# A hybrid decoder layer on one core: half-height score products, a predicated copy, half-width value products, and new homes for three buffers

## The chip, the cores and the metric

One of the eight cores of a Trainium2 chip runs the whole layer. The metric is device time in microseconds; lower is better. TensorE multiplies 128-row by 128-column weight tiles with streams of up to 512 columns into PSUM; VectorE, ScalarE and GpSimd work on 128 partitions; SyncE's queue issues most transfers.

## The reference, cut to what matters

The layer has two sub-layers over 1024 positions of width 1024. The first takes one input projection, and gives part of its columns to four mLSTM heads (a convolution of width 4, then chunks of a matrix memory) and part to eight attention heads of 64 dimensions in two key/value groups, with rotary, a window of 128 positions and a learned sink per head. The second is a gated MLP with a convolution of width 3. Both are modulated by six vectors, which are products of a 1024-vector with `w_ada`, 24 MB of weights in 48 chunks of 128 columns. All of it is float32.

```
kband = concatenate([previous key block, key block])      # 256 keys for 128 queries
s = einsum('bnqgrd,bnkgd->bngrqk', qb, kband) / sqrt(64)
s = where((rel >= 0) & (rel < 128), s, -inf)               # rel = query - key position
m = maximum(max(s), sink);  p = exp(s - m)
p = p / (sum(p) + exp(sink - m))
o = einsum('bngrqk,bnkgd->bnqgrd', p, vband)
```

For each query exactly 128 of the 256 keys are valid: key column c of the previous block where c is above the query's row, and of the own block where it is not.

## The kernel before, in words

The program is written in Python over a tile framework. A planner, with a timeline of its own, sets the order of each engine's instructions; buffers are taken from pools, and an instruction waits until the buffer that it writes is free.

The work goes in this order. `h_chunk` computes the modulated input. A first pass over it gives keys and values (`pkv`) and half the mLSTM values. `kv_evac` applies rotary to the keys, transposes them and splits them into a rounded part `khi` and a rest `klo`, so that three float32r products (`mm3`, lines 88 to 90) give a float32-like product. `token_group(4, ...)` gives values and gates. `att_group(6, 0)` and `att_group(8, 1)` each project queries for eight blocks of 128 positions, four heads at a time, and run `att_front` and, two blocks later, `att_back`. Behind them `conv_chunk` projects q and k of each mLSTM head into `ubq` and `ubk` and convolves them on VectorE, and `ml_head` runs the chunks. Then come the gate `o_group`, the output projection and the MLP.

In `att_front` the queries of two heads (one of each key/value group) lie above each other in 128 rows. `khi` and `klo` have two planes, one a group, each with zeros in the other group's 64 rows. One product of 128 rows and 2 x 256 columns therefore gives the scores of both heads against both key blocks. ScalarE copies them to `raw`, GpSimd clears the invalid half of each block (lines 367 and 368), and VectorE adds the two blocks into `sm` (line 369). Maximum, exponential and sum follow.

In `att_back` the probabilities are transposed. One product takes the whole transposed block with the previous block's values, a second one the part that belongs to the own block with the difference of the two blocks' values (`vdf`). Both have the values of both groups, 128 columns, and line 399 picks the group's 64.

Two buffers meet here. `ada_bg` loads a chunk of `w_ada` during the attention into the buffer `ub` of the pool `wp`, one buffer, and multiplies it on VectorE (line 174); the same buffer later holds `ubq`. `ubk` is in the pool `lp`, which takes the memory of the attention's pools after `ap_.release()` and `kp.release()`.

Of the kernel before, what the change touches and what calls it, by code (L numbers as in the profile page):

```python
# [10 lines left out]
F32 = mybir.dt.float32  # L11
F32R = mybir.dt.float32r
# [6 lines left out]
P = 128  # L19
# [38 lines left out]
def layer_kernel(  # L58
# [19 lines left out]
    def f(ap):  # L78
        return ap.bitcast(F32)
# [7 lines left out]
    def mm3(ps, lh, ll, rh, rl, first, last):  # L87
        T.matmul(ps, lh, rh, start=first, stop=False)  # L88
        T.matmul(ps, lh, rl, start=False, stop=False)  # L89
        T.matmul(ps, ll, rh, start=False, stop=last)  # L90
# [57 lines left out]


    cb = adap.tile([P, D], F32, name="cb")  # L150
    kp = tc.alloc_tile_pool(name="keys", bufs=1, side="right")
    khi = kp.tile([P, 2, S], F32R, name="khi")
    klo = kp.tile([P, 2, S], F32R, name="klo")
    G.memset(f(khi), 0.0)
    G.memset(f(klo), 0.0)
    ap0 = tc.alloc_tile_pool(name="start", bufs=1, side="right")
    xT = ap0.tile([P, KD, S], F32, name="xT")
    crow, cth = (ap0.tile([P, D], F32, tag=f"w{i}", name=n)[0:1, :] for i, n in enumerate(("crow", "cth")))
# [13 lines left out]
    def ada_chunk(j, w):  # L172
        nc.sync.dma_start(w, w_ada[j * P : (j + 1) * P, :])
        V.scalar_tensor_tensor(w, w, 1.0, cb, op0=ALU.mult, op1=ALU.mult, accum_out=mod[:, j : j + 1])  # L174
# [75 lines left out]

    ada_left = list(range(16, 48))

    def ada_bg(pool=None):
        j = ada_left.pop(0)
        ada_chunk(j, pool.tile([P, D], F32, tag="w", bufs=2, name=f"ada{j}") if pool else wp.tile([P, 4 + S], F32, tag="ub", name=f"ada{j}")[:, :D])

    def token_group(u, n, evac):
        (h0, l0), (h1, l1) = units[u], units[u + 1]
# [58 lines left out]
    def kv_evac(b, ps):  # L317
        kr = ap_.tile([P, 256], F32, tag="qr", bufs=2, name=f"kr{b}")
        rope(kr[:, :P].rearrange("p (h t f) -> p h t f", h=2, t=2),
             ps[:, :P].rearrange("p (h t f) -> p h t f", h=2, t=2), b, 2)  # L320
        A.copy(vat[:, b, :], ps[:, P : 2 * P])
        if b:
            V.tensor_tensor(vdf[:, b, :], ps[:, P : 2 * P], vat[:, b - 1, :], op=ALU.subtract)
        pk = pB(f"pk{b}")
        T.transpose(pk[:, :P], kr[:, :P], ident)
        ts = slice(b * P, (b + 1) * P)
        for g in range(2):
            r = slice(64 * g, 64 * g + 64)
            A.copy(khi[r, g, ts], pk[r, :P])
            V.tensor_tensor(klo[r, g, ts], pk[r, :P], f(khi[r, g, ts]), op=ALU.subtract)  # L330

    rsta = cp.tile([P, NB], F32, name="rsta")

    def att_front(gi, b, ps):
        qr = ap_.tile([P, 256], F32, tag="qr", bufs=2, name=f"qr{gi}_{b}")
        rope(qr.rearrange("p (h t f) -> p h t f", h=4, t=2),
             ps[:, :256].rearrange("p (h t f) -> p h t f", h=4, t=2), b, 4)
        pq = pB(f"pq{gi}_{b}")
        for i in range(2):
            T.transpose(pq[:, i * P : (i + 1) * P], qr[:, i * P : (i + 1) * P], ident)  # L340
        qhi = ap_.tile([P, 256], F32R, tag="qhi", bufs=2, name=f"qhi{gi}_{b}")
        qlo = ap_.tile([P, 256], F32R, tag="qlo", bufs=2, name=f"qlo{gi}_{b}")
        A.activation(qhi, pq[:, :256], AF.Copy, scale=0.125)
        V.scalar_tensor_tensor(qlo, pq[:, :256], 0.125, f(qhi), op0=ALU.mult, op1=ALU.subtract)
        den = ap_.tile([P, 4], F32, tag="den", bufs=3, name=f"den{gi}_{b}")
        ngm = ap_.tile([P, 4], F32, tag="ngm", bufs=3, name=f"ngm{gi}_{b}")
        mx = ap_.tile([P, 4], F32, tag="mx", bufs=3, name=f"mx{gi}_{b}")
        es = ap_.tile([P, 4], F32, tag="es", bufs=3, name=f"es{gi}_{b}")

        sinks = rw[:, 8:16].rearrange("p (v j) -> p j v", v=2)[:, 2 * gi : 2 * gi + 2, :]  # L350
        nsk = nsink.rearrange("p (v j) -> p j v", v=2)[:, 2 * gi : 2 * gi + 2, :]

        sm = ap_.tile([P, 4, P], F32, tag="sm", bufs=4, name=f"sm{gi}_{b}")
        kn = P if b == 0 else 2 * P
        ks = slice((b + 1) * P - kn, (b + 1) * P)
        for i in range(2):
            ps_s = pA(f"s{gi}_{b}_{i}")[:, : 2 * kn].rearrange("p (v k) -> p v k", v=2)
            mm3(ps_s, qhi[:, i * P : (i + 1) * P], qlo[:, i * P : (i + 1) * P], khi[:, :, ks], klo[:, :, ks], True, True)
            si = sm[:, 2 * i : 2 * i + 2, :]
            if b == 0:  # L360
                A.copy(si, ps_s)
                G.affine_select(si, si, pattern=[[0, 2], [-1, P]], compare_op=ALU.is_ge, fill=NEG, base=0, channel_multiplier=1)
            else:
                raw = ap_.tile([P, 2, 2 * P], F32, tag="sr", bufs=3, name=f"sr{gi}_{b}_{i}")
                A.copy(raw, ps_s)
                old, new = raw[:, :, :P], raw[:, :, P:]
                G.affine_select(old, old, pattern=[[0, 2], [1, P]], compare_op=ALU.is_ge, fill=0.0, base=-1, channel_multiplier=-1)
                G.affine_select(new, new, pattern=[[0, 2], [-1, P]], compare_op=ALU.is_ge, fill=0.0, base=0, channel_multiplier=1)
                V.tensor_tensor(si, old, new, op=ALU.add)
        V.tensor_reduce(mx, sm, axis=AX.X, op=ALU.max)  # L370
        V.scalar_tensor_tensor(ngm.rearrange("p (j v) -> p j v", v=2), mx.rearrange("p (j v) -> p j v", v=2), -1.0, nsk, op0=ALU.mult, op1=ALU.min)  # L371
        for i in range(4):
            A.activation(sm[:, i, :], sm[:, i, :], AF.Exp, bias=ngm[:, i : i + 1], accum_out=den[:, i : i + 1])  # L373
        V.tensor_tensor(es.rearrange("p (j v) -> p j v", v=2), ngm.rearrange("p (j v) -> p j v", v=2), sinks, op=ALU.add)
        A.activation(es, es, AF.Exp)
        V.tensor_tensor(den, den, es, op=ALU.add)
        V.reciprocal(den, den)
        return sm, den

    def att_back(gi, b, sm, den):  # L380
        pt = pB(f"pt{gi}_{b}").rearrange("p (a b) -> p a b", a=4)
        for i in range(4):
            T.transpose(pt[:, i, :], sm[:, i, :], ident)

        pT = ap_.tile([P, 4, P], F32, tag="pT", bufs=4, name=f"pT{gi}_{b}")
        A.copy(pT, pt)
        pTs = [(pT, vat[:, max(b - 1, 0), :])]
        if b:
            pN = ap_.tile([P, 4, P], F32, tag="pT", bufs=4, name=f"pN{gi}_{b}")
            G.affine_select(pN, pT, pattern=[[0, 4], [1, P]], compare_op=ALU.is_ge, fill=0.0, base=0, channel_multiplier=-1)  # L390
            pTs.append((pN, vdf[:, b, :]))
        po = pC(f"po{gi}_{b}")
        for i in range(4):
            for n, (pT, va) in enumerate(pTs):
                T.matmul(po[:, i * P : (i + 1) * P], pT[:, i, :], va, start=n == 0, stop=n == len(pTs) - 1)

        base = ATT0 + gi * 128
        for v in range(2):
            V.tensor_tensor(
                mix[b][:, base + v * 256 : base + v * 256 + 128].rearrange("p (j d) -> p j d", j=2),  # L400
                po.rearrange("p (j v d) -> p j v d", j=2, v=2)[:, :, v, 64 * v : 64 * v + 64],
                bc(den.rearrange("p (j v) -> p j v", v=2)[:, :, v], 2, [P, 2, 64]),
                op=ALU.mult,
            )
        if gi == 1:
            sq = ap_.tile([P, 4, P], F32, tag="sm", bufs=4, name=f"asq{b}")
            A.activation(sq.rearrange("p a b -> p (a b)"), mix[b][:, ATT0:], AF.Square, accum_out=ssq[:, b : b + 1])
            rstd_of(rsta[:, b : b + 1], ssq[:, b : b + 1], 512)
            G.tensor_scalar(mix[b][:, ATT0:], mix[b][:, ATT0:], rsta[:, b : b + 1], 0.0, op0=ALU.mult, op1=ALU.add)
# [10 lines left out]
    def v_gates(b, ps):  # L420
        v_evac(b, 0, ps[:, :256])
        A.copy(gates.rearrange("p (g b) -> p g b", g=8)[:, :, b], ps[:, 256:264])
        ada_bg()

    for b in range(NB):
        G.memset(mix_v(b)[:, :, HD : HD + 1], vscale)
# [4 lines left out]
    def att_group(u, gi):  # L431
        pending = []

        def ev(b, ps):
            pending.append((gi, b, *att_front(gi, b, ps)))
            ada_bg()
            if len(pending) > 2:
                att_back(*pending.pop(0))

        token_group(u, 256, ev)  # L440
        while pending:
            att_back(*pending.pop(0))
# [84 lines left out]
    def conv_chunk(u, ch, name):  # L527
        hi, lo = units[u]
        hi = hi[:, :1024].rearrange("p (k n) -> p k n", k=8)
        lo = lo[:, :1024].rearrange("p (k n) -> p k n", k=8)  # L530
        ub = (wp if name[0] == "q" else lp).tile([P, 4 + S], F32, tag="ub", bufs=1, name=f"ub{name}")
        V.memset(ub[:, 0:4], 0.0)
        for t in range(2):
            ps = mm(f"cv{name}_{t}")
# [654 lines left out]
```

## Time and profile before

| | |
|---|---|
| median of 3 runs | 1161.43 us (1159.47 to 1161.55) |
| the profiled execution | 1161.49 us, span 1159.1 us |
| TensorE busy | 1114.8 us, 96% |
| VectorE busy | 858.7 us, 74% |
| ScalarE busy | 578.4 us, 50% |
| GpSimd busy | 212.4 us, 18% |
| moved by DMA | 144.72 MB |

The span is the part of an execution that the profiler saw. A row of the timeline says when an instruction started and how long it took; matmuls overlap their neighbours, so their pace is read from one start to the next. PEld is TensorE's weight load. Brackets hold the idle time ahead of an instruction and what ended it.

### The profile page before, as it was taken

Reading aid. Unit: us, or ns where it says so; the run is one execution under the profiler, and the core shown is the slowest. Engines: PE = TensorE matmul, PEld = TensorE weight load, DVE = VectorE, ACT = ScalarE, POOL = GpSimd, SP = SyncE. Lnnn points to the kernel's source line nnn. Section 1 sums busy time; section 2 is a strip of 40 time slices with the busy share of each in tenths; the row PEclk is TensorE's granted clock in tenths of the full one; section 3 lists DMA queues with packets and bytes.
Section 4 is the critical chain, followed back from the end, with each engine's and each line's share of the span. In section 5 each row is a group of like instructions: output and inputs, shape, how many; then the busy total and the mean of one; then the engine's idle time right before and its main releaser. Section 6 shows DMA issues by size and latency. Waiting matters only on the chain.

```text
span 1159.1 us, 16041 instructions
## 1 busy us (share of the span) xinstructions
PE 1114.8 (96%) x5811; PEld 942.3 (81%) x5811; DVE 858.7 (74%) x1529; ACT 578.4 (50%) x1184; POOL 212.4 (18%) x300
## 2 busy tenths in 40 slices
PE   5899989988999999999999999999999999999997
PEld 3898989877899988887788888888888888787885
DVE  6956877459776545789987797878878775787666
ACT  6543456544554535566554454545454555345452
POOL 3011555665577400000000000000000000000021
PEclk9899999999999999999999999999999999999998
DMA  9654330133110512333332333133223358553545
GB/s 345 243 193 157 108 101 2 56 127 109 55 55 1 182 57 89 108 111 105 113 105 77 118 118 107 67 118 118 93 81 109 114 188 287 192 172 119 172 117 200
DMA packets 54161, 144.72 MB, mean 125 GB/s; under 512 B 5265, under 2 KB 5569, under 8 KB 54082
## 3 DMA queue, kind: packets, MB, share of 16 engines
q1 hardware_dynamic: 52208, 138.19, 35.4%
q10 hardware_dynamic: 1874, 5.51, 1.2%
q8 instruction: 45, 0.74, 0.3%
q14 instruction: 34, 0.28, 0.1%
HBM read 115.09 MB, written 28.60 MB: 124 GB/s over the span
## 4 chain that ended last, share of the span: by engine, by line
PE 68%; DVE 6%; DMA 2%; issue 1%; POOL 1%; ACT 1%; SPq 0%; DVEq 0%; POOLq 0%; ACTq 0%
PE X L858 7%; PE X L857 7%; PE X L856 7%; PE Y L858 4%; PE Y L856 4%; PE Y L857 4%; PE y L88 3%; PE y L90 3%; PE y L89 3%; PE Z L858 1%; PE Z L856 1%; PE Z L857 1%; PE dx L1029 1%; PE dx L1028 1%; PE dxu L1030 1%; PE dx L1030 1%
## 5 line engine op out<-in xcount | busy, mean ns | idle before, releaser
L93 POOL TENSOR_SCALAR rsb<-ssb 128x1 f32<-128x1 f32 x4 | 2.3, 584 | 611.0 <-ACT junk L1081 610.8
L174 DVE SCALAR_TENSOR_TENSOR ada<-ada,cb 128x1024 f32<-128x1024 f32 x48 | 65.2, 1365 | 29.0 <-DMA ada<-in_w_ada_dram 29.0
L856 PE MATMUL X<-S,wl 128*128 128x512 f32 x156 | 62.4, 400 | 0.0
L858 PE MATMUL X<-S,wl 128*128 128x512 f32 x156 | 61.9, 396 | 0.0
L857 PE MATMUL X<-S,wl 128*128 128x512 f32 x156 | 61.7, 395 | 0.0
L866 DVE SCALAR_TENSOR_TENSOR yg<-ug,cv,yg 128x1023 f32<-128x1023 f32 (+1 forms) x44 | 56.4, 1281 | 5.7 <-ACT yg L863 5.7
L85 ACT CAST wl<-T 128x512 fp32r<-128x512 f32 x41 | 25.5, 621 | 66.4 <-PE X L857 62.6
L866 DVE SCALAR_TENSOR_TENSOR yv<-uv,cv,yv 128x1023 f32<-128x1023 f32 (+1 forms) x44 | 56.3, 1279 | 1.9 <-ACT yv L863 1.9
L85 ACT CAST w<-T 128x512 fp32r<-128x512 f32 x47 | 29.1, 623 | 40.8 <-PE Z L858 34.7
L85 DVE TENSOR_TENSOR w<-T,w 128x512 fp32r<-128x512 f32 x47 | 32.1, 688 | 16.6 <-ACT w L85 16.6
L85 DVE TENSOR_TENSOR A<-ra,A 128x512 fp32r<-128x512 f32 x46 | 31.6, 687 | 17.0 <-ACT A L85 16.9
L910 DVE TENSOR_TENSOR uv<-q,X 128x512 f32<-128x512 f32 x22 | 15.1, 686 | 38.4 <-PE X L858 38.4
L85 ACT CAST B<-rb 128x512 fp32r<-128x512 f32 x44 | 27.2, 619 | 31.3 <-DMA rb<-in_w_down_dram 13.4
L85 ACT CAST A<-ra 128x512 fp32r<-128x512 f32 x46 | 28.5, 620 | 28.6 <-PE dxu L1030 14.1
L373 ACT ACTIVATE sm<-sm,ngm 128x128 f32<-128x128 f32 x64 | 24.9, 391 | 27.7 <-DVE ngm L371 27.1
L85 DVE TENSOR_TENSOR B<-rb,B 128x512 fp32r<-128x512 f32 x44 | 30.2, 687 | 9.7 <-ACT B L85 9.1
L85 ACT CAST wl<-fu 128x512 fp32r<-128x512 f32 x21 | 13.0, 621 | 47.5 <-PE Y L857 44.5
L858 PE MATMUL Y<-S,wl 128*128 128x512 f32 x92 | 36.4, 396 | 0.0
L856 PE MATMUL Y<-S,wl 128*128 128x512 f32 x92 | 36.4, 395 | 0.0
L857 PE MATMUL Y<-S,wl 128*128 128x512 f32 x92 | 36.2, 394 | 0.0
L857 PEld LDWEIGHTS X<-S,wl 128*128 128x128 f32 x156 | 29.3, 188 | 7.6 <-issue 0.5
L856 PEld LDWEIGHTS X<-S,wl 128*128 128x128 f32 x156 | 29.3, 188 | 7.5 <-issue 0.5
(621 smaller groups left out, 4040.5 us busy)
## 6 DMA issues: line engine op xcount, KB each, us to landing
ada<-in_w_ada_dram SPq DMA_DIRECT2D x48, 512.0 KB, 4.5
ra<-a_dram SPq DMA_DIRECT2D x30, 512.0 KB, 3.8
fu<-in_w_up_dram SPq DMA_DIRECT2D x26, 512.0 KB, 3.5
a_dram<-yg SPq DMA_DIRECT2D x22, 512.0 KB, 3.8
rb<-in_w_down_dram SPq DMA_DIRECT2D x44, 256.0 KB, 4.0
fu_False<-in_w_up_dram SPq DMA_DIRECT2D x18, 512.0 KB, 3.6
a_dram<-s SPq DMA_DIRECT2D x11, 512.0 KB, 5.3
x<-in_x_dram SPq DMA_DIRECT2D x8, 512.0 KB, 7.3
```

Source lines behind the costliest of these rows:

```text
L85: return A.copy(hi, src), eng.tensor_tensor(lo, src, f(hi), op=ALU.subtract)
L88: T.matmul(ps, lh, rh, start=first, stop=False)
L89: T.matmul(ps, lh, rl, start=False, stop=False)
L90: T.matmul(ps, ll, rh, start=False, stop=last)
L174: V.scalar_tensor_tensor(w, w, 1.0, cb, op0=ALU.mult, op1=ALU.mult, accum_out=mod[:, j : j + 1])
L373: A.activation(sm[:, i, :], sm[:, i, :], AF.Exp, bias=ngm[:, i : i + 1], accum_out=den[:, i : i + 1])
L856: T.matmul(ps, w[:, 0, ks], a[:, 0, k, :], start=st, stop=False, skip_group_check=True)
L857: T.matmul(ps, w[:, 0, ks], a[:, 1, k, :], start=False, stop=False, skip_group_check=True)
L858: ends = T.matmul(ps, w[:, 1, ks], a[:, 0, k, :], start=False, stop=en, skip_group_check=True)
L866: V.scalar_tensor_tensor(t[:, sh:], src[:, : S - sh], w(tap), t[:, sh:], op0=ALU.mult, op1=ALU.add)
L910: V.tensor_tensor(uv[:, 512:], p5, px_, op=ALU.add)
L1030: ends = T.matmul(ps[tb], a[:, 1, ts], w[:, 0], start=False, stop=last and r == NP - 1, skip_group_check=True)
```

## The change

The keys lose their second plane and the zeros: `khi` and `klo` are 128 x 1024, with group 0 in the upper 64 rows and group 1 in the lower. Scores are taken by products of 64 rows, one per group, 256 columns (128 in the first block), into two PSUM tiles, one per group. The own block's scores are copied to `sm`, and a predicated copy writes the previous block's over them where the constant mask `later` is set. The value products take only their group's 64 columns. The chunks of `w_ada` during the attention go to two buffers of the pool `ap_`. `ubk` is one tile of the pool `adap`, there from the start.

```
-    khi = kp.tile([P, 2, S], F32R, name="khi")
-    klo = kp.tile([P, 2, S], F32R, name="klo")
-    G.memset(f(khi), 0.0)
-    G.memset(f(klo), 0.0)
+    ubk = adap.tile([P, 4 + S], F32, name="ubk")
+    khi = kp.tile([P, S], F32R, name="khi")
+    klo = kp.tile([P, S], F32R, name="klo")
...
-    def ada_bg(pool=None):
+    def ada_bg(pool):
         j = ada_left.pop(0)
-        ada_chunk(j, pool.tile([P, D], F32, tag="w", bufs=2, ...) if pool else wp.tile([P, 4 + S], F32, tag="ub", ...)[:, :D])
+        ada_chunk(j, pool.tile([P, D], F32, tag="w", bufs=2, name=f"ada{j}"))
...
-        for g in range(2):
-            r = slice(64 * g, 64 * g + 64)
-            A.copy(khi[r, g, ts], pk[r, :P])
-            V.tensor_tensor(klo[r, g, ts], pk[r, :P], f(khi[r, g, ts]), op=ALU.subtract)
+        split(khi[:, ts], klo[:, ts], pk[:, :P])
+    later = ap_.tile([P, P], F32, name="later")
+    G.memset(later, 1.0)
+    G.affine_select(later, later, pattern=[[1, P]], compare_op=ALU.is_ge, fill=0.0, base=-1, channel_multiplier=-1)
...
+        pss = [pA(f"s{gi}_{b}_{v}")[:, : 2 * kn].rearrange("p (j k) -> p j k", j=2) for v in range(2)]
         for i in range(2):
-            ps_s = pA(f"s{gi}_{b}_{i}")[:, : 2 * kn].rearrange("p (v k) -> p v k", v=2)
-            mm3(ps_s, qhi[:, i * P : (i + 1) * P], qlo[:, i * P : (i + 1) * P], khi[:, :, ks], klo[:, :, ks], True, True)
+            for n, (qt, kt) in enumerate(((qhi, khi), (qhi, klo), (qlo, khi))):
+                for v in range(2):
+                    r = slice(64 * v, 64 * v + 64)
+                    T.matmul(pss[v][:, i, :], qt[r, i * P : (i + 1) * P], kt[r, ks], start=n == 0, stop=n == 2)
...
-                raw = ap_.tile([P, 2, 2 * P], F32, tag="sr", bufs=3, name=f"sr{gi}_{b}_{i}")
-                A.copy(raw, ps_s)
-                old, new = raw[:, :, :P], raw[:, :, P:]
-                G.affine_select(old, old, ...)
-                G.affine_select(new, new, ...)
-                V.tensor_tensor(si, old, new, op=ALU.add)
+                A.copy(si, pss[v][:, :, P:])
+                V.copy_predicated(si, bc(later.bitcast(mybir.dt.uint32), 1, [P, 2, P]), pss[v][:, :, :P])
...
-                T.matmul(po[:, i * P : (i + 1) * P], pT[:, i, :], va, ...)
+                T.matmul(po[:, i * 64 : (i + 1) * 64], pt_[:, i, :], va[:, v], ...)
...
-        ub = (wp if name[0] == "q" else lp).tile([P, 4 + S], F32, tag="ub", bufs=1, name=f"ub{name}")
+        ub = wp.tile([P, 4 + S], F32, tag="ub", bufs=1, name=f"ub{name}") if name[0] == "q" else ubk
```

## Rows read from the trace of the kernel before

**Rows 1.** The page, busy time of each engine (share of the span) xinstructions

```profile
PE 1114.8 (96%) x5811; PEld 942.3 (81%) x5811; DVE 858.7 (74%) x1529; ACT 578.4 (50%) x1184; POOL 212.4 (18%) x300
```

**Rows 2.** Waits of TensorE from 110 to 300 us: total, times, longest

```profile
PE cvq L88 <- ACT ubk L537: 5.2, 2, 3.2
...
PE tg L88 <- DVE rb L313: 1.9, 1, 1.9
PE s L90 <- DVE qlo L344: 1.1, 2, 0.8
```

**Rows 3.** Windows: stretch, busy time of each engine, granted clock, DMA share

```profile
261.00:290.00 29.00, 26.01 (x127) 20.94 (x126) 27.42 (x33) 12.32 (x19) 17.17 (x10) 1.00 0.33 109
```

**Rows 4.** Groups by line and form, 104 to 240 us: busy us, mean ns

```profile
L365 ACT COPY sr<-s 128x512 f32<-128x512 f32 x28 | 15.5, 578 | 7.4 <-PE s L90 6.6 <-POOL sr L368 0.6
L367 POOL TENSOR_SCALAR_AFFINE_SELECT sr<-sr 128x256 f32<-128x256 f32 x28 | 14.1, 503 | 19.8 <-ACT sr L365 19.8
L369 DVE TENSOR_TENSOR sm<-sr 128x256 f32<-128x256 f32 x28 | 14.0, 506 | 7.1 <-POOL sr L368 6.0 <-ACT pT L386 1.1
...
L344 DVE SCALAR_TENSOR_TENSOR qlo<-pq,qhi 128x256 fp32r<-128x256 f32 x16 | 6.5, 413 | 1.6 <-ACT qhi L343 1.6
```

**Rows 5.** Timeline of TensorE, 220 to 222 us: start, us, instruction

```profile
220.16 0.39 PE L395 MATMUL po<-vdf,pN 128*128 128x128 f32 x2
220.38 0.39 PE L395 MATMUL po<-vat,pT 128*128 128x128 f32 x2
...
221.53 0.39 PE L88 MATMUL s<-khi,qhi 128*128 128x512 f32 x1
221.76 0.39 PE L89 MATMUL s<-klo,qhi 128*128 128x512 f32 x1
```

**Rows 6.** Timeline of TensorE, 189.4 to 190.7 us

```profile
189.41 0.28 PE L90 MATMUL tg<-w8hi,hTlo 128*128 128x256 f32 x1
...
189.70 0.22 PE L511 MATMUL pg<-ident,crow 32*128 32x32 f32 x1
189.76 0.38 PE L515 MATMUL pg<-gt,ones 32*128 32x32 f32 x2
189.99 0.38 PE L516 MATMUL pg<-gt,ones 32*128 32x32 f32 x2
...
190.63 0.40 PE L89 MATMUL s<-klo,qhi 128*128 128x512 f32 x1
```

**Rows 7.** Timeline of TensorE, 183.9 to 184.9 us

```profile
183.91 0.28 PE L88 MATMUL tg<-w8hi,hThi 128*128 128x256 f32 x1
184.12 0.24 PE L511 MATMUL pg<-ident,arow 32*128 32x32 f32 x1
...
184.52 0.28 PE L90 MATMUL tg<-w8hi,hTlo 128*128 128x256 f32 x1
...
184.87 0.28 PE L90 MATMUL tg<-w8hi,hTlo 128*128 128x256 f32 x1
```

**Rows 8.** Timeline of TensorE, one block's scores in parts

```profile
158.16 0.40 PE L89 MATMUL s<-klo,qhi 128*128 128x512 f32 x1
...
159.87 0.47 PE L88 MATMUL s<-khi,qhi 128*128 128x512 f32 x1
```

**Rows 9.** Waits of VectorE from 80 to 246 us: total, times, longest

```profile
DVE ada L174 <- DMA ada<-in_w_ada_dram: 19.3, 14, 3.5
```

**Rows 10.** Timeline of VectorE, 110 to 114 us

```profile
110.48 1.23 DVE L174 SCALAR_TENSOR_TENSOR ada<-ada,cb 128x1024 f32<-128x1024 f32 x1 [2.30 <-DMA ada<-in_w_ada_dram]
...
113.60 0.42 DVE L311 TENSOR_TENSOR ra<-tg,trig 128x256 f32<-128x256 f32 x1
```

**Rows 11.** Windows, columns as above (PEclk follows the five engines)

```profile
115.40:118.90 3.50, 3.50 (x19) 3.50 (x18) 2.97 (x10) 0.00 (x0) 0.88 (x2) 0.52 0.58 192
...
248.50:252.00 3.50, 3.50 (x10) 2.73 (x9) 2.63 (x4) 0.07 (x1) 0.00 (x0) 0.52 0.97 392
```

**Rows 12.** Timeline of ScalarE, 273 us

```profile
273.69 0.57 ACT L537 COPY ubk<-cvk 128x512 f32<-128x512 f32 x1
```

More of the change, by code (lines that the diff above doesn't have):

```diff
@@ L251, in layer_kernel @@
     ada_left = list(range(16, 48))
-    def ada_bg(pool=None):
+    def ada_bg(pool):
         j = ada_left.pop(0)
-        ada_chunk(j, pool.tile([P, D], F32, tag="w", bufs=2, name=f"ada{j}") if pool else wp.tile([P, 4 + S], F32, tag="ub", name=f"ada{j}")[:, :D])
+        ada_chunk(j, pool.tile([P, D], F32, tag="w", bufs=2, name=f"ada{j}"))
     def token_group(u, n, evac):
@@ L355, in att_front @@
         ks = slice((b + 1) * P - kn, (b + 1) * P)
+        pss = [pA(f"s{gi}_{b}_{v}")[:, : 2 * kn].rearrange("p (j k) -> p j k", j=2) for v in range(2)]
         for i in range(2):
-            ps_s = pA(f"s{gi}_{b}_{i}")[:, : 2 * kn].rearrange("p (v k) -> p v k", v=2)
-            mm3(ps_s, qhi[:, i * P : (i + 1) * P], qlo[:, i * P : (i + 1) * P], khi[:, :, ks], klo[:, :, ks], True, True)
-            si = sm[:, 2 * i : 2 * i + 2, :]
+            for n, (qt, kt) in enumerate(((qhi, khi), (qhi, klo), (qlo, khi))):
+                for v in range(2):
+                    r = slice(64 * v, 64 * v + 64)
+                    T.matmul(pss[v][:, i, :], qt[r, i * P : (i + 1) * P], kt[r, ks], start=n == 0, stop=n == 2)
+        smv = sm.rearrange("p (j v) k -> p v j k", v=2)
+        for v in range(2):
+            si = smv[:, v]
             if b == 0:
-                A.copy(si, ps_s)
+                A.copy(si, pss[v])
                 G.affine_select(si, si, pattern=[[0, 2], [-1, P]], compare_op=ALU.is_ge, fill=NEG, base=0, channel_multiplier=1)
             else:
-                raw = ap_.tile([P, 2, 2 * P], F32, tag="sr", bufs=3, name=f"sr{gi}_{b}_{i}")
-                A.copy(raw, ps_s)
-                old, new = raw[:, :, :P], raw[:, :, P:]
-                G.affine_select(old, old, pattern=[[0, 2], [1, P]], compare_op=ALU.is_ge, fill=0.0, base=-1, channel_multiplier=-1)
-                G.affine_select(new, new, pattern=[[0, 2], [-1, P]], compare_op=ALU.is_ge, fill=0.0, base=0, channel_multiplier=1)
-                V.tensor_tensor(si, old, new, op=ALU.add)
+                A.copy(si, pss[v][:, :, P:])
+                V.copy_predicated(si, bc(later.bitcast(mybir.dt.uint32), 1, [P, 2, P]), pss[v][:, :, :P])
         V.tensor_reduce(mx, sm, axis=AX.X, op=ALU.max)
@@ L391, in att_back @@
             pTs.append((pN, vdf[:, b, :]))
-        po = pC(f"po{gi}_{b}")
+        po = pC(f"po{gi}_{b}")[:, :256]
         for i in range(4):
-            for n, (pT, va) in enumerate(pTs):
-                T.matmul(po[:, i * P : (i + 1) * P], pT[:, i, :], va, start=n == 0, stop=n == len(pTs) - 1)
+            v = slice(64 * (i % 2), 64 * (i % 2) + 64)
+            for n, (pt_, va) in enumerate(pTs):
+                T.matmul(po[:, i * 64 : (i + 1) * 64], pt_[:, i, :], va[:, v], start=n == 0, stop=n == len(pTs) - 1)
         base = ATT0 + gi * 128
@@ L400, in att_back @@
                 mix[b][:, base + v * 256 : base + v * 256 + 128].rearrange("p (j d) -> p j d", j=2),
-                po.rearrange("p (j v d) -> p j v d", j=2, v=2)[:, :, v, 64 * v : 64 * v + 64],
+                po.rearrange("p (j v d) -> p j v d", j=2, v=2)[:, :, v, :],
                 bc(den.rearrange("p (j v) -> p j v", v=2)[:, :, v], 2, [P, 2, 64]),
@@ L422, in v_gates @@
         A.copy(gates.rearrange("p (g b) -> p g b", g=8)[:, :, b], ps[:, 256:264])
-        ada_bg()
+        ada_bg(ap_)
     for b in range(NB):
@@ L435, in ev @@
             pending.append((gi, b, *att_front(gi, b, ps)))
-            ada_bg()
+            ada_bg(ap_)
             if len(pending) > 2:
```

## The prediction

> **What bounds the kernel now.** I read the page first: TensorE is busy 96% of the span, VectorE 74% [rows 1], so work that TensorE loses or gains in a dense stretch shows in the time almost one for one. The 40 slices put the attention between about 80 and 246 us. There the question is how much of TensorE's time is work and how much is waiting, so I read its waits from 110 to 300 us: of seven groups three can be touched by this change, 5.2 us for `ubk`, 1.9 us for `rb` and 1.1 us for `qlo` [rows 2]. The stage behind the attention is the reverse case: from 261 to 290 us VectorE is busy 27.42 of 29 us and TensorE 26.01 [rows 3]. The chain of waits starts there too, with modulation chunks and the convolutions on VectorE. So up to 246 us TensorE's work sets the pace, and for some 40 us behind it VectorE's queue does. I work in TensorE's time, and then ask what the second stage gives back. The profiled execution took 1161.49 us, 2.4 us more than its span and 0.06 us above the median of the three runs; I add to 1161.5.
>
> **Edits off TensorE.** ScalarE copies 256 score columns in place of 512 (28 of 578 ns before), GpSimd loses 56 selects of about half a microsecond, VectorE has 28 predicated copies for 28 adds of 506 ns [rows 4]. No row shows a predicated copy. A VectorE instruction that reads 256 columns from PSUM takes 413 ns [rows 4]; the upper bound is twice that, were mask and data read one after the other. I take 0.41, since it moves the same columns: 11.6 us against 14.2, at most 23. At 0.41 it frees a little of an engine that is not the bound here. At 0.83 it adds 9 us over 16 blocks, some 0.6 us each, beside the roughly 8 us of a block ((246 - 115) / 16): hidden as well. A new wait: the two score banks are now freed by VectorE instead of ScalarE, and behind them only the next block's scores queue. The merged key split drops eight small instructions each from ScalarE and VectorE, the removed clears and the new mask are GpSimd work with nothing behind it on the path. I put all this at 0.
>
> **Value products, 64 columns for 128.** There are 120 products, each two instructions on TensorE. A pair starts 0.22 us after the pair before, so 0.11 us an instruction [rows 5]. If columns set that, half the columns would save 120 x 0.11 = 13 us. But the two small f32 products of the gate stage have 32 columns and still start 0.23 us a pair, 0.115 an instruction [rows 6]. With a quarter of the columns and no saving, the load of 128 weight columns sets the pace, and the change keeps those loads. I take 0; the 13 us are excluded by that row.
>
> **Score products.** Before, 14 blocks have 6 matmuls of 512 columns, 0.23 us apart [rows 5], more closely 0.2325 over a run: 84 x 0.2325 = 19.5 us. After, 168 matmuls of 256 columns, in 84 pairs on the two halves of the rows. A 256-column matmul takes 0.117 us ((184.87 - 184.52) / 3) [rows 7]. No row shows two row halves at work, so the pair has two bounds: 0.1175 if they run together, about 0.23 if one after the other. Together: 84 x 0.1175 = 9.9 us, a gain of 9.7. One after the other at the weight load's 0.115: 168 x 0.115 = 19.3, no gain. The two first blocks have 24 matmuls of 128 columns for 12 of 256 at 0.1175 (1.4 us): together 12 x 0.115 = 1.4, no change; apart 2.8, a loss of 1.4. I take together: the two halves use different rows of the array and different banks, and the loop places them back to back.
>
> The Trainium skill (TensorE: Matmul & The Clock Gate, Part 3: Packing small matmuls) says that matmuls in distinct row groups start about 4 ns apart and run at the same time, and gives 3.07 times the rate for four of 32 rows. By it the pair costs one matmul; no run here shows it.
>
> **The price of changing the array's shape.** Only two places in this stretch use fewer than 128 rows, and both cost more than their matmuls. At 183.91 us a projection matmul is followed by one 32-row transpose and another projection, and the fourth starts at 184.52: 0.61 us, where two projection matmuls (0.235) and the transpose (0.07, by 189.70 to 189.76 in the other place) make 0.31 [rows 6, 7]. So 0.30 us go in and out. The second visit runs from 189.41 to 190.63 us, 1.22 us; one projection matmul, two transposes, four 32-column matmuls and one score matmul make 0.12 + 0.14 + 0.46 + 0.23 = 0.95, so 0.27 [rows 6]. Before, all scores use 128 rows and pay none of it. After, each run of scores between other matmuls pays it once. In the timeline the 16 blocks' scores stand in 30 runs, because the last of the three terms waits for `qlo` and other matmuls are put between, as at 158.16 and 159.87 [rows 8]. So 30 x 0.30 = 9.0 us; 16 runs would be 4.8, 45 would be 13.5.
>
> The Trainium skill (TensorEngine Tiling (Array Packing), Key Properties) states that a change of tiling mode drains the engine, which speaks against this change. The trace agrees, with its 0.30 and 0.27 us; the sum uses these.
>
> **Modulation chunks and `ubk`.** With one buffer VectorE stood 19.3 us in 14 places for chunk transfers [rows 9]. One of them costs TensorE: the chunk at 110.48 us was 2.30 us late, the rotary work of the first query block came behind it at 113.60 [rows 10], and TensorE waited 1.9 us for it [rows 2]. The granted clock then fell to 0.52 in 115.4 to 118.9, which is the 1.2 GHz level [rows 11]; 16 matmuls at 0.213 us for 0.1175 there cost some 1.6 us more. With a second buffer the transfer is under way earlier: 1.9 + 1.6 = 3.5 us. The wait for `qlo` behind a late chunk is worth 0.8 of its 1.1. Bounds are 0 and that full 4.3.
>
> `ubk` no longer waits for the attention's memory, so the 3.2 us stall at 245 us goes, and with it the slow clock of 248.5 to 252 (3.5 us at 0.52, about 1.6 lost) [rows 2, 11]. What is late next: the second key projection is evacuated at 273.69 us, after VectorE's convolution chain [rows 12], and TensorE waited 2.0 us for that [rows 2]. VectorE's chain starts when the attention's memory is free, which `ubk` does not move. TensorE arrives 4.8 us earlier and waits about 4 us longer there. I leave 0.9. Stalls in all: 3.5 + 0.8 + 0.9 = 5.2 us.
>
> **The sum.** Scores -9.7, shape changes +9.0, stalls -5.2: -5.9 us, so 1155.6. Its own range: 16 runs give 1151.4, 45 give 1160.1, and without the stalls' gain 1160.8.
>
> **Rivals.**
> First, the row halves do not run together. Weights of both halves are loaded one after the other at 0.115 us, and 168 small matmuls cost what 84 large ones did: -0.2 + 1.4 + 9.0 - 5.2 = +5.0, 1166.5 us, slower. It decides from a pair price of 0.19 us on, for then 84 x 0.19 + 9.0 - 5.2 equals the 19.5 us of before. For it speaks that 32-row loads show no cheaper pace than 128-row matmuls [rows 6]; against it, that these stood on the same rows.
> The Trainium skill (TensorE: Matmul & The Clock Gate, LDWEIGHTS) gives a load as columns / 1.2 ns whatever the rows, about 107 ns here; if such loads queue, this rival's time follows. The trace agrees on the size with its 0.115.
> Second, the stalls come back. TensorE's lead is lost at the convolutions, and a chunk earlier is a chunk beside other VectorE work: -9.7 + 9.0, 1160.8 us, no change that can be told. For it speaks VectorE's 27.42 of 29 us [rows 3].
> Third, the runs close up, as GpSimd no longer stands between scores and softmax: 16 visits, -9.7 + 4.8 - 5.2 = -10.1, 1151.4 us, or the visit is cheaper for 64 rows than for 32.
>
> **How the numbers follow.** The forecast case gets 0.43, the first rival 0.32, the second 0.13, the third 0.12. The likeliest gives 1155.6. About 0.2% (2.3 us) is what three runs can tell. Of the forecast, nearly all is faster; the third rival is faster; the first is slower but for a tenth faster and a fifth within 0.2%; the second is mostly the same. That gives faster 0.51, same 0.19, slower 0.30. Both signs hold weight, so the range goes from just past the third rival to just past the first: 1149 to 1168; the forecast's own is 1151 to 1161.
>
> **What would show it.** Right: score matmuls of 64 rows in pairs, starts within 0.02 us of each other or 0.12 us a pair; 0.15 us more at each edge of a run; value products still 0.11 us an instruction; no wait of TensorE for `ubk` at 245 us, but one of 6 us near 270; no fall of the clock at 115 us. Wrong: pairs at 0.23 us; edges without a gap; value products at half the pace; a wait of TensorE for the predicated copy; or an order of instructions behind 246 us in which VectorE's chain is itself shorter or longer.

## The result, and the profile after

| | before | after |
|---|---|---|
| median of 6 runs | 1161.47 us (1159.47 to 1163.45) | 1155.91 us (1152.94 to 1157.41) |
| ratio, 95% interval | | 0.9949 [0.9931, 0.9967] |
| profiled execution, span | 1161.49 us, 1159.1 us | 1152.94 us, 1150.9 us |

The forecast was 1155.6 us. The profiled execution of after is the fastest of its six, so the two traces differ by 8.5 us where the medians differ by 5.6. They part in the middle: the stretch from the first value and gate product (`tg`, at 80.4 us before and 80.2 after) to the last `tot` of the mLSTM (376.6 and 368.7) is 7.7 us shorter, and from the last product of the output projection to TensorE's last matmul it is 650.7 and 651.0 us.

The page of after, busy time of each engine, answers to [rows 1]:

```profile
PE 1114.0 (97%) x5907; PEld 941.0 (82%) x5907; DVE 849.6 (74%) x1521; ACT 570.5 (50%) x1176; POOL 184.3 (16%) x244
```

TensorE has 96 instructions more and about the same busy time; GpSimd lost its selects. One run of scores, timeline of TensorE of after (start, duration, instruction; x2 is two matmuls taken together):

```profile
125.03 0.28 PE L89 MATMUL tg<-w6lo,hThi 128*128 128x256 f32 x1
125.24 0.39 PE L362 MATMUL s<-khi,qhi 64*128 64x256 f32 x2
125.46 0.29 PE L362 MATMUL s<-klo,qhi 64*128 64x256 f32 x2
125.58 0.29 PE L362 MATMUL s<-khi,qlo 64*128 64x256 f32 x2
125.69 0.29 PE L362 MATMUL s<-khi,qhi 64*128 64x256 f32 x2
125.81 0.30 PE L362 MATMUL s<-klo,qhi 64*128 64x256 f32 x2
125.92 0.30 PE L362 MATMUL s<-khi,qlo 64*128 64x256 f32 x2
126.15 0.39 PE L90 MATMUL tg<-w6hi,hTlo 128*128 128x256 f32 x1
126.38 0.28 PE L88 MATMUL tg<-w6hi,hThi 128*128 128x256 f32 x1
```

Once the run has begun, its pairs step by 0.11 to 0.12 us: the two halves work together. From 125.03 to 126.38 are 1.35 us, where two `tg` matmuls (0.235) and six pairs (6 x 0.1175 = 0.705) make 0.94, so the visit costs 0.41. It lies in four starts, 0.21 to 0.23 us after the one before in place of 0.117: two at the way in, two at the way out.

Not every run has pairs. In eight of the 28 runs, two of six matmuls and six of two, the planner put the matmuls of one half alone, and they step by the same 0.12 us without a partner:

```profile
178.62 0.38 PE L362 MATMUL s<-khi,qhi 64*128 64x256 f32 x1
178.84 0.28 PE L362 MATMUL s<-klo,qhi 64*128 64x256 f32 x1
178.96 0.28 PE L362 MATMUL s<-khi,qlo 64*128 64x256 f32 x1
```

The other half's six follow from 180.20 us on. That is 12 steps more than pairs would take, 1.4 us.

The value products with 64 columns still start 0.22 us apart, as in [rows 5]; timeline of TensorE of after:

```profile
146.79 0.39 PE L398 MATMUL po<-vat,pT 128*128 128x64 f32 x2
147.01 0.39 PE L398 MATMUL po<-vdf,pN 128*128 128x64 f32 x2
147.24 0.39 PE L398 MATMUL po<-vat,pT 128*128 128x64 f32 x2
```

The join, groups by line and form of after, 104 to 240 us (busy us, mean ns, idle time before), against L365, L367 and L369 in [rows 4]:

```profile
L371 DVE COPY_PREDICATED sm<-later,s 128x256 f32<-128x256 uint32 x28 | 11.3, 438 | 8.9 <-ACT sm L370 8.5
...
L370 ACT COPY sm<-s 128x256 f32<-128x256 f32 x28 | 9.0, 370 | 6.8 <-PE s L362 6.5
```

The predicated copy takes 0.44 us and ScalarE's copy 0.37 for 0.58; VectorE's wait is for the own block's scores. The waits of TensorE from 110 to 300 us, which answer to [rows 2], and VectorE's wait for chunks from 80 to 246 us, which answers to [rows 9]:

```profile
PE mS L575 <- issue: 5.4, 1, 5.4
PE tg L88 <- DVE lgB L458: 1.9, 1, 1.9
```

```profile
DVE ada L173 <- DMA ada<-in_w_ada_dram: 8.2, 10, 1.7
```

The `ubk` and `qlo` waits are gone; VectorE waits 8.2 us for chunks in place of 19.3. The 5.4 us stand ahead of 264.69 us, and end with VectorE's last step on `zk`; timelines of VectorE and TensorE of after:

```profile
262.16 1.21 DVE L173 SCALAR_TENSOR_TENSOR ada<-ada,cb 128x1024 f32<-128x1024 f32 x1
...
263.36 1.23 DVE L547 SCALAR_TENSOR_TENSOR zk<-zk,cyk 128x1024 f32<-128x1024 f32 x1
```

```profile
264.69 0.77 PE L575 MATMUL mS<-zq,zk 128*128 128x128 f32 x2 [5.43 <-issue]
```

A 1.9 us wait near 112 us stayed, with another releaser, and so did the slow clock behind it; windows of after (columns as in [rows 3, 11]):

```profile
112.50:116.50 4.00, 4.00 (x21) 4.00 (x22) 2.78 (x9) 0.00 (x0) 1.23 (x4) 0.57 0.85 284
264.50:268.50 4.00, 3.81 (x18) 3.84 (x19) 3.89 (x7) 1.24 (x1) 0.00 (x0) 0.50 0.18 74
```

After 1.9 us without a matmul the granted clock was 0.57 for 4 us, and after 5.4 us it was 0.50, the 1.2 GHz level.

### The profile page after: what moved, and what is told of

Same layout as the page of the kernel before. It is cut to its first block, busy times and chain, and to the rows that moved or that the text cites. A ratio compares the mean times of both kernels' runs of the same rounds, so it can differ in the third digit from the quotient of the medians.

```text
span 1150.9 us, 16161 instructions
## 1 busy us (share of the span) xinstructions
PE 1114.0 (97%) x5907; PEld 941.0 (82%) x5907; DVE 849.6 (74%) x1521; ACT 570.5 (50%) x1176; POOL 184.3 (16%) x244
## 4 chain that ended last, share of the span: by engine, by line
PE 80%; DVE 8%; DMA 6%; issue 2%; ACT 2%; POOL 2%; SPq 0%; DVEq 0%; POOLq 0%; ACTq 0%
PE X L860 7%; PE X L859 7%; PE X L858 7%; PE Y L860 4%; PE Y L858 4%; PE Y L859 4%; DMA ada<-in_w_ada_dram 3%; PE y L88 3%; PE y L90 3%; PE y L89 3%; DVE ada L173 3%; PE tg L90 2%; PE tg L89 2%; PE tg L88 2%; PE po L398 2%
## 5 line engine op out<-in xcount | busy, mean ns | idle before, releaser
L85 DVE TENSOR_TENSOR w<-T,w 128x512 fp32r<-128x512 f32 x47 | 32.2, 688 | 16.6 <-ACT w L85 16.6
L858 PEld LDWEIGHTS X<-S,wl 128*128 128x128 f32 x156 | 29.4, 188 | 7.5 <-issue 0.5
L859 PEld LDWEIGHTS X<-S,wl 128*128 128x128 f32 x156 | 29.3, 188 | 7.6 <-issue 0.5
L860 PEld LDWEIGHTS X<-S,wl 128*128 128x128 f32 x156 | 29.3, 188 | 7.1
```

The lines of the kernel that those rows point to most:

```text
L85: return A.copy(hi, src), eng.tensor_tensor(lo, src, f(hi), op=ALU.subtract)
L858: T.matmul(ps, w[:, 0, ks], a[:, 0, k, :], start=st, stop=False, skip_group_check=True)
L859: T.matmul(ps, w[:, 0, ks], a[:, 1, k, :], start=False, stop=False, skip_group_check=True)
L860: ends = T.matmul(ps, w[:, 1, ks], a[:, 0, k, :], start=False, stop=en, skip_group_check=True)
```

## The experiments

Twelve runs of kernels, all made from the changed one (the unchanged one among them). Ratios are to the kernel before, which ran beside them.

| run | median us | ratio, 95% | work | waits, slow clock |
|---|---|---|---|---|
| (before) | 1161.47 | 1 | 397.3 | 22.1 |
| (after) | 1155.91 | 0.9949 [0.9931, 0.9967] | 397.2 | 13.9 |
| again | 1154.3 | 0.9937 [0.992, 0.9953] | 397.5 | 13.5 |
| samehalf | 1164.47 | 1.0033 [1.0021, 1.0045] | 405.6 | 19.2 |
| apart | 1161.12 | 0.9996 [0.9984, 1.0008] | 397.7 | 18.0 |
| val128 | 1156.25 | 0.995 [0.9937, 0.9962] | 394.7 | 19.7 |
| lofirst | 1152.7 | 0.9923 [0.9909, 0.9938] | 393.3 | 18.7 |
| ubk_lp | 1153.96 | 0.9952 [0.9936, 0.9968] | 397.1 | 14.1 |
| ada_one | 1160.69 | 0.9996 [0.9982, 1.0011] | 396.7 | 19.8 |
| rows128_one | 1165.33 | 1.0047 [1.0033, 1.0061] | 397.5 | 23.1 |
| selects_one | 1174.29 | 1.0121 [1.0104, 1.0137] | 397.0 | 34.7 |
| selects_ubk | 1171.34 | 1.0087 [1.0071, 1.0102] | 397.1 | 32.2 |
| chunks_early | 1156.58 | 0.9961 [0.9946, 0.9976] | 396.6 | 15.9 |
| early_lofirst | 1153.05 | 0.9931 [0.9915, 0.9947] | 394.7 | 15.4 |

The last two columns are a ledger of one trace each, in us, from the first `tg` matmul to the last one of the output projection. Each matmul is charged its pace (0.1175 us for 256 columns, 0.2325 for 512, 0.11 for each instruction of a value product or transpose), and a run of scores all that lies between its neighbours: that is the work. What is left between starts is waits and slow clock. The figures are good to about 1 us. A profiled execution may stand 2 us or more from its median, so the ledger tells where time went, and the ratio how much.

**again**, the changed kernel unchanged, as the mark for what stands beside it.

> The changed kernel once more, on the chip of the other three. Theory: 5.6 us under the kernel before (1155.9 against 1161.5), within 2 us; pairs of 64-row score matmuls 0.12 us apart. Rival: the six runs so far drew a good lot and the difference is under 2 us.

It came out at 0.9937, inside the first interval.

**samehalf**, whether the halves' working together is the gain.

```
-                    r = slice(64 * v, 64 * v + 64)
+                    r = slice(0, 64)
```

> Both score matmuls of a pair use the upper 64 rows, so the second key/value group's own scores are left out (it gets the first group's). The number of matmuls, their columns, the banks and everything behind them stay as in the changed kernel. Theory (the pairs gain because two row halves work at once): the two of a pair now queue on one half, 12 score matmuls take about 12 x 0.117 = 1.41 us for 0.705, and 84 pairs cost 84 x 0.1175 = 9.9 us more of TensorE; the time is 1164 to 1166 us against the changed kernel's 1155. Rival (the scores sit in slack, and the gain is from the chunk buffers alone): the time stays within 2 us of the changed kernel's.

The timeline of TensorE of this kernel, with its run of scores before the next `tg`:

```profile
129.23 0.38 PE L362 MATMUL s<-khi,qhi 64*128 64x256 f32 x1
129.46 0.28 PE L362 MATMUL s<-klo,qhi 64*128 64x256 f32 x1
...
130.28 0.40 PE L362 MATMUL s<-klo,qhi 64*128 64x256 f32 x2
130.51 0.40 PE L362 MATMUL s<-khi,qlo 64*128 64x256 f32 x2
130.84 0.39 PE L90 MATMUL tg<-w6hi,hTlo 128*128 128x256 f32 x1
```

On one half a pair takes 0.23 us (130.28 to 130.51) for 0.117. All runs of scores together, their neighbours' own paces taken off and a start between two close runs counted once, take 32.7 us for 23.0, 9.7 more against 9.9 expected, and the ratio rises by 0.0084 over the first measurement of after, by 0.0096 over again: 9.8 to 11.1 us. This is the first rival's kernel, and it is slower than before. The theory held, its range of 1164 to 1166 us too.

**apart**, the three products of the upper half and then the three of the lower.

```
-            for n, (qt, kt) in enumerate(((qhi, khi), (qhi, klo), (qlo, khi))):
-                for v in range(2):
-                    r = slice(64 * v, 64 * v + 64)
+            for v in range(2):
+                r = slice(64 * v, 64 * v + 64)
+                for n, (qt, kt) in enumerate(((qhi, khi), (qhi, klo), (qlo, khi))):
```

> The six score matmuls of a head pair go in another order: three of the upper row half, then three of the lower, so that neighbours share their rows. Theory (two halves at once are what the 64-row form gains): 168 matmuls at about 0.115 us in place of 84 pairs, 9.7 us more TensorE work, about 1165 us. Rival (TensorE has slack in this stretch, and the gain is from the buffers): 1156 us, no change.

The time rose by 6.8 us over again, but not by what was to be tested: the halves ran together all the same. In three of its five runs of twelve the program built from this kernel holds the products exactly as written, three of the upper half and then three of the lower, twice. This is the first of them; timeline of TensorE of this kernel:

```profile
125.10 0.40 PE L362 MATMUL s<-khi,qhi 64*128 64x256 f32 x2
125.33 0.29 PE L362 MATMUL s<-klo,qhi 64*128 64x256 f32 x2
125.45 0.29 PE L362 MATMUL s<-khi,qlo 64*128 64x256 f32 x2
125.57 0.29 PE L362 MATMUL s<-khi,qhi 64*128 64x256 f32 x2
```

Each line is two matmuls of the same term, 0.01 us apart. The profile doesn't name the half, but two matmuls of one half would stand 0.12 us apart or more (samehalf). So the lower half's first product, fourth in the program, started with the upper half's first and ahead of its second. The expectation failed at its premise, that neighbours in the queue must be of different halves. The work in the ledger is the same (397.7), and the last `tot` is at 368.6 us as in after; the time came behind it, where the gate's and the last mLSTM products stand in another order with more waits (from the last `tot` to the last product of the output projection 127.5 us for 122.7). So this run says nothing of what the overlap is worth (samehalf does); it shows that a changed order far behind an edit moves the time by several us.

**val128**, the value products with 128 columns again.

> Value products with 128 columns again, all else as changed. Theory (the weight load sets the pace, 0.11 us an instruction at 32, 64 and 128 columns): no change, 1156 us within 1.5. Rival (columns set the pace): up to 13 us more, 1169 us.

0.995: no change beside after and again that the intervals tell, and far from the rival's 13 us. Columns do not set the pace of these products, as the forecast took from [rows 6].

**lofirst**, the score terms in the order that puts the late operand `qlo` first.

```
-            for n, (qt, kt) in enumerate(((qhi, khi), (qhi, klo), (qlo, khi))):
+            for n, (qt, kt) in enumerate(((qlo, khi), (qhi, khi), (qhi, klo))):
```

> The term with the queries' rest comes first, so that a block's scores start only when everything is there and stand in one run. Theory (each visit of the 64-row shape costs 0.3 to 0.4 us): runs fall from 28 to about 17, 3 to 4 us less, about 1152 us. Rival (edges cost nothing, or what they cost is waiting in disguise): same as the changed kernel, or up to 1 us more because the first two terms start later.

Runs went from 28 to 21 (17 were expected) and their sum from 23.0 to 19.3 us, as the price of a visit wants. (The 24.3 us in the expectation of early_lofirst count the start between two close runs twice.) The time fell by 1.6 us beside again, which the intervals do not tell from nothing: in the ledger the work is 4 us lower than in after, and the waits are 5 us longer.

**ubk_lp**, `ubk` back in the pool `lp`.

> ubk goes back to the pool that waits for the attention's memory; all else as changed. Theory of the prediction: TensorE's lead is lost again at VectorE's convolutions, 0.9 us, so 1157 us. Rival (the lead is kept, 3.2 us of waiting and 1.6 of slow clock): 1160 to 1161 us.

0.9952, or 0.3 to 1.7 us above the two measurements of the changed kernel. That excludes the rival's 4.8 us; 0.9 and nothing can't be told apart. The trace has no wait of TensorE for `ubk`, and the wait for `zk` is 5.3 us as in after (5.4).

**ada_one**, the chunks in one buffer again, all else as changed.

```
-        ada_chunk(j, pool.tile([P, D], F32, tag="w", bufs=2, name=f"ada{j}"))
+        ada_chunk(j, pool.tile(... tag="w", bufs=2 ...) if pool is not ap_ else wp.tile([P, 4 + S], F32, tag="ub", ...)[:, :D])
```

> The chunks of w_ada go to one buffer again, the one that ubq uses later; all else as changed. Theory of the prediction: the second buffer is worth 4.3 us, so 1160 us. Rival (the trace after the change still has the 1.9 us wait and the slow clock at 110 us, and VectorE's queue is full of chunks there either way): under 2 us, 1156 to 1158.

0.9996: the gain is gone, 5.5 to 6.8 us by the ratios. The timeline of VectorE and of TensorE of this kernel (in brackets the idle time ahead and what ended it):

```profile
106.97 1.23 DVE L173 SCALAR_TENSOR_TENSOR ada<-ada,cb 128x1024 f32<-128x1024 f32 x1 [2.91 <-DMA ada<-in_w_ada_dram]
...
111.89 1.23 DVE L173 SCALAR_TENSOR_TENSOR ada<-ada,cb 128x1024 f32<-128x1024 f32 x1 [3.69 <-DMA ada<-in_w_ada_dram]
113.04 0.08 DVE L173 DVE_READ_ACCUMULATOR ada<-ada,cb 128x1 f32 x1
113.04 1.22 DVE L85 TENSOR_TENSOR w7lo<-w7raw,w7hi 128x1024 fp32r<-128x1024 f32 x1
```

```profile
114.32 0.58 PE L89 MATMUL tg<-w7lo,hThi 128*128 128x256 f32 x1 [3.46 <-DVE w7lo L85]
```

A chunk 3.69 us late holds the weight split behind it, and TensorE waits 3.46 us for that. With two buffers VectorE waits only 0.16 us for a chunk in the same stretch, 106 to 113 us, of after:

```profile
107.84 1.23 DVE L173 SCALAR_TENSOR_TENSOR ada<-ada,cb 128x1024 f32<-128x1024 f32 x1 [0.16 <-DMA ada<-in_w_ada_dram]
...
109.13 1.22 DVE L85 TENSOR_TENSOR w8lo<-w8raw,w8hi 128x1024 fp32r<-128x1024 f32 x1
110.27 1.22 DVE L173 SCALAR_TENSOR_TENSOR ada<-ada,cb 128x1024 f32<-128x1024 f32 x1
...
112.24 0.18 DVE L458 TENSOR_SCALAR lgB<-lgA 128x32 f32<-128x32 f32 x1
```

The 1.9 us that TensorE still waits there are work now: two chunks and a split stand ahead of `lgB` in VectorE's queue. In the ledger waits and slow clock are 5.9 us more in ada_one than in after. By TensorE's waits 1.6 us are at this place, 1.8 ahead of key transposes between 83 and 99 us, and 0.8 less ahead of the mLSTM; the rest is in smaller waits and slow clock.

**rows128_one**, ada_one with the 128-row score products and the zero planes again; the predicated copy and the 64-column value products stay.

> As ada_one, and the scores go back to 128 rows, two zeroed key planes and 512 columns, with the predicated copy kept (two planes do not fit beside the two chunk buffers). To be held against ada_one. Theory: the overlap's 9.7 us and the price of the shape's 28 visits, 8 to 10 us, nearly cancel: within 2 us of ada_one. Rival (the visits' price is hidden): 8 to 10 us more than ada_one.

4.6 us over ada_one, between the theory's 2 and the rival's 8: both missed. The two score forms cost TensorE 23.5 us in 31 runs here and 22.0 in 27 runs in ada_one; most of the difference lies in the last column.

**selects_one**, ada_one with the old join: the copy of 512 columns, two selects, the addition.

```
-                A.copy(si, pss[v][:, :, P:])
-                V.copy_predicated(si, bc(later...), pss[v][:, :, :P])
+                raw = ap_.tile([P, 2, 2 * P], F32, tag="sr", bufs=3, ...)
+                A.copy(raw, pss[v])
+                old, new = raw[:, :, :P], raw[:, :, P:]
+                G.affine_select(old, ...); G.affine_select(new, ...)
+                V.tensor_tensor(si, old, new, op=ALU.add)
```

> As ada_one, and the two key blocks are joined as before, with a 512-column copy, two GpSimd selects and an add in place of the predicated copy. To be held against ada_one. Theory: off the path, within 1 us. Rival (the shorter chain from score to softmax is what took the waits out of the attention, 12.4 us of lost TensorE time before and 3.1 after): 3 to 6 us more than ada_one.

13.6 us over ada_one, where at most 1 was expected and 3 to 6 by the rival: both missed. Timeline of TensorE of this kernel:

```profile
252.86 0.40 PE L90 MATMUL cvq<-hThi,w12lo 128*128 128x512 f32 x1
253.09 0.33 PE L402 MATMUL po<-vat,pT 128*128 128x64 f32 x2
...
254.60 0.39 PE L402 MATMUL po<-vdf,pN 128*128 128x64 f32 x2
267.24 0.79 PE L88 MATMUL cvk<-hThi,w13hi 128*128 128x512 f32 x1 [12.26 <-ACT ubq L543]
```

The planner had put the next `q` projection ahead of the attention's last value products, and TensorE then stood 12.3 us for its evacuation to `ubq`. The last value product is at 254.6 us; in ada_one it is at 237.8.

**selects_ubk**, the same with `ubk` in the pool `lp`, to see whether the early `q` projection was the cause.

> The 64-row scores with the old join (a copy of 512 columns, two selects on GpSimd, an addition), one chunk buffer, and ubk back in the pool that waits for the attention's memory. It differs from the kernel that measured 1174.3 us by ubk's place alone. Theory (with ubk free from the start TensorE's queue ran the first q projection ahead of the attention's tail, and both banks then waited 12.3 us for ubq's evacuation): the wait goes down to about that of the kernel before, and the time is 1160 to 1165. Rival (the longer join itself delays the attention's last blocks): within 2 us of 1174.

The 12.3 us wait went down to 3.1, now for `ubk`, and the time only from 1.0121 to 1.0087, 3.9 us. Both missed, the rival by less. Waits of TensorE, 78 to 300 us, and one group by line and form, 104 to 252 us, of this kernel:

```profile
PE cvq L88 <- ACT ubk L542: 3.1, 1, 3.1
PE tg L89 <- DVE w7lo L85: 3.1, 1, 3.1
...
PE po L401 <- ACT pT L391: 2.0, 2, 1.1
PE po L401 <- POOL pN L395: 1.9, 2, 1.5
```

```profile
L374 DVE TENSOR_TENSOR sm<-sr 128x256 f32<-128x256 f32 x28 | 15.3, 547 | 13.1 <-POOL sr L373 13.1
```

VectorE stands 13.1 us for GpSimd's selects, 6.0 in the kernel before [rows 4]. That would follow if the two score banks are full at nearly the same time in the 64-row form, so that their four selects queue at once. The timelines agree: the four selects of a block stand in one row, 0.36 us from start to start, in 11 of 14 blocks here and in 6 of 14 before. That this sets TensorE's loss was not tested by itself.

A large part of the loss is the clock. The last three blocks' value products have no projections between them here, TensorE stood 1.08 and 1.54 us in waits at 239 and 241 us, and then the granted clock fell for 21 us; window of this kernel, columns as in [rows 3, 11]:

```profile
241.00:262.00 21.00, 16.51 (x62) 14.53 (x63) 8.66 (x20) 6.58 (x19) 7.24 (x12) 0.51 0.27 99
```

Pairs of value products started 0.43 us apart there for 0.22, and projections 0.43 for 0.23. By these paces some 6 us were lost, an estimate, where the kernel before lost some 1.4 in the 3.5 us of [rows 11].

**chunks_early**, the eight chunks of the mLSTM stage moved into the second half of the attention.

```
-            ada_bg(ap_)
+            for _ in range(1 + gi):
+                ada_bg(ap_)
...
-        ada_bg(lp)
```

> The eight modulation chunks that VectorE multiplies in the mLSTM stage are moved into the second half of the attention, two a block there. Theory (behind the attention VectorE's queue of convolutions and chunks sets the pace, which is where TensorE waited 5.4 us at 259 us): 8 x 1.2 = about 10 us leave that queue, TensorE's wait there shrinks to under 2 us, and the time falls by 4 to 8 us, to 1147 to 1151. Rival (the attention's blocks have no room for a second chunk, or the wait only moves to the next evacuation): within 2 us of the changed kernel, or slower by what TensorE waits in the attention.

1156.58 us: the theory fell, and the rival's 2 us hold. Waits of TensorE, 110 to 300 us, of this kernel:

```profile
PE cvk L88 <- ACT ubq L540: 1.7, 1, 1.7
...
PE tg L89 <- DVE w9lo L85: 1.4, 1, 1.4
...
PE cvq L88 <- ACT ubk L540: 0.5, 1, 0.5
```

The wait of 5.4 us shrank to 1.7 and 0.5 as expected, and the ledger's waits and slow clock are 15.9 us for 13.9 all the same: new ones of 0.6 to 1.4 us stand in the attention and later in the mLSTM chunks, where TensorE now arrives ahead of VectorE and ScalarE.

**early_lofirst**, both of the last edits.

> The eight chunks moved into the second half of the attention, and the score terms in the order that puts the late operand qlo first, so that a block's scores are not parted (21 runs of scores for 28). Theory: the shape changes cost 5 us less in sum (19.3 for 24.3 with the order alone) and are no longer eaten by the wait behind the attention: 3 to 5 us below the kernel with the chunks alone, 1143 to 1148. Rival (the lead is lost at the next wait for VectorE, as it was with the order alone, which measured 1.6 us): within 2 us of the chunks alone.

0.9931, 3.5 us below the chunks alone, as the theory had it, though not in its range of 1143 to 1148 us, and no better than the order alone (0.9923). No version beat the changed kernel by more than the measurement can tell.

## Why the prediction was right, point by point

- **The sum.** 1155.6 forecast, 1155.9 and 1154.3 measured. The gain lies in the waits, as forecast: the ledger's work is 397.3 us before and 397.2 after, its waits and slow clock 22.1 and 13.9. But they went at other places than the forecast's 5.2 us. The 3.5 us near 112 us are still there, as 1.9 us of waiting and the same fall of the clock. The 6.2 us at `ubk` and `ubq` became 5.4. Beside the 1.1 us for `qlo` there went 1.6 us ahead of 110 us (for `kr` and `gates`), and two groups of the view of [rows 2] that the forecast passed over:

```profile
PE po L395 <- ACT pT L386: 2.4, 2, 1.7
...
PE po L395 <- POOL pN L390: 0.7, 2, 0.4
```

  They are waits of the value products for the chain behind the scores. To that extent the number came out by luck.
- **Pairs at 0.1175 us.** Right: steps of 0.11 to 0.12 us in a run of pairs, and samehalf shows the other price, 0.23 a pair and 1164.5 us. The Trainium skill (TensorE: Matmul & The Clock Gate, Part 3: Packing small matmuls) has matmuls of distinct row groups run at the same time; the trace agrees, with pairs that step by 0.117 us. That each half always has its partner was not so: 12 lone steps cost 1.4 us.
- **The price of a visit.** Right in kind, somewhat too small. The runs of scores take 23.0 us in all. The steps, 12 of 128 columns at 0.115 us and 96 of 256 at 0.1175, make 12.7, so 28 visits cost 10.3 us, 0.37 each, for 30 x 0.30 = 9.0. By the same measure the scores before took 23.2, of which 20.9 are the matmuls' paces and the rest mostly waits for `qlo`: against the paces they are 2.1 us dearer, and not 0.7 cheaper. Runs of 12 matmuls with 256 columns pay 0.27 to 0.41. The Trainium skill (TensorEngine Tiling (Array Packing), Key Properties) has a change of tiling mode drain the engine; the trace agrees, with four starts of 0.21 to 0.23 us a visit.
- **Value products at 0.** Right: 0.22 us a product before and after, and val128 changes nothing that can be told.
- **The second chunk buffer.** Forecast 4.3 us, measured 5.5 to 6.8 with ada_one. That a late chunk holds up what TensorE needs is shown there, at other places than forecast: the wait of 1.9 us near 112 us and the slow clock behind it are still in after, for work in place of a transfer. The term counted only the waits that the view of before named; the changed kernel with one buffer has others, 3.5 us for `w7lo` and 1.8 ahead of key transposes.
- **`ubk`.** Forecast 0.9, measured 0.3 to 1.7 (ubk_lp), which is not told from nothing. That the wait would move behind VectorE's chain was right: 5.4 us ahead of 264.7, forecast as 6 near 270.
- **Edits off TensorE at 0.** The step that the runs do not bear out. The predicated copy takes 0.44 us, near the lower bound of 0.41, and VectorE has room. But with 64-row scores the old join costs 13.6 us (selects_one), of which 3.9 go with `ubk`'s place. The forecast costed the join by engines' busy time, and left out TensorE's waits for what comes behind it. The price belongs to no edit alone: with 128-row scores and one chunk buffer the old join (the kernel before, 1161.5 us) is faster than the new one (rows128_one, 1165.3, which differs besides by `ubk`'s place and the value columns), and with 64 rows it is slower (1174.3 and 1171.3 against 1160.7).
- **The total does not split into terms.** The kernel before, ada_one and apart take the same 1161 us, and rows128_one, which undoes more than ada_one, takes 1165. Undone one by one the parts are worth 5.5 to 6.8 (chunks), 4.6 (64 rows, with one chunk buffer) and 13.6 (join, likewise): far more than the 5.6 us of the whole. All but samehalf and the reordered scores have the same work within 0.8 us (val128 2.5 less), and differ in waits and slow clock, which come out anew with the planner's order after each edit. That the sum came out within 1 us is therefore in part luck of the orders that the two kernels got. Of the 10 us between before and selects_ubk, which differ by the 64-row scores with their keys and by the value columns, some 4.6 are slow clock by the estimate above; why the planner left that tail without projections, and what the rest is, was not settled.

## What to carry to other kernels

Two row halves at work together halve the price of a score product, but a visit to the other array shape costs 0.27 to 0.41 us. By these numbers a run of six pairs saves about 0.34 us net (6 x 0.2325 = 1.395 for 0.705 + 0.35), and a run of one or two pairs, which saves 0.12 or 0.23 us, loses. Look at the planner's order, too, for matmuls that stand without their partner. Where TensorE had 96% of the span, added work cost its full time (samehalf, 9.7 us of work, 9.8 to 11.1 of time), while removed work was mostly given back in waits for other engines (lofirst, 4 us of work, 1.6 of time, which is not told from nothing). Ask of each wait on the bounding engine whether the edit touches the chain behind it, and not only whether the engines of that chain have room. Ask of a late transfer what stands behind its reader in the queue: a second buffer here was worth more than the waits that TensorE's view named.

## What the runs showed of the hardware

- The two row halves went on like two queues: in apart, in a run that the program holds as three products of the upper half and then three of the lower, the products of the two halves started in pairs 0.01 us apart.
- A change between 128 and 64 rows showed in four starts, two on each side of the run, at 0.21 to 0.23 us in place of 0.117 (after, 125 us).
- In selects_ubk, behind waits of 1.08 and 1.54 us, the granted clock was 0.51 for 21 us (241 to 262 us), and TensorE's steps were nearly twice as long.
- A predicated copy of 128 x 256 from PSUM took 438 ns on VectorE (after, mean of 28), about the 413 of an instruction that reads the same columns without a mask [rows 4].
